# Seven block products in place of eight in an MLP's first matrix product

## The chip, the cores and the metric

The kernel runs on 1 of the 8 cores of one Trainium2 chip. The metric is the device time of one execution in microseconds (us), the median of several runs. TensorE is called PE in the profile, with PEld for its weight loads; VectorE is DVE, ScalarE is ACT, GpSimd is POOL, and SyncE, which issues DMAs, is SP. ACT issues DMAs too.

## The reference

One inference step of one layer over 640 rows (128 context and 512 latent tokens) of 1024 columns, in float32:

```
h    = rmsnorm(x, norm1_g) * (1 + scale1) + shift1
mix  = concat(hgrn2, gla, rglru, short_conv mixers of h @ w_in) @ w_out
x    = x + gate1 * mix
h2   = rmsnorm(x, norm2_g) * (1 + scale2) + shift2
ff   = square(relu(h2 @ mlp_w1)) @ mlp_w2      # 1024 -> 4096 -> 1024
x    = x + gate2 * ff
y    = rmsnorm(x, final_norm_g)
```

The outputs are y and the final states of three mixers. The change is in the part from `gate1 * mix` to the end, above all in `h2 @ mlp_w1`.

## The kernel before

**How a float32 product is formed.** Each operand is split into a rounded part `hi` (type float32r, made by ACT as a copy) and the rest `lo` (made by DVE as a subtraction), and a product is three matmuls, hi*hi, hi*lo and lo*hi, added in PSUM. `prep` (line 108) does this for weights: a DMA from SP brings 128x2048 raw values (1 MB), ACT writes `hi`, DVE writes `lo`. One matmul has a 128x128 stationary operand and 320 or 512 moving columns.

**The stretch before the MLP** (lines 893 to 963). The output projection `op` is formed by row tiles t = 0 to 4 of 128 rows, 48 matmuls each (`out_mm`). For each t, DVE multiplies by the gate (`gm`, line 939) and adds to the residual row `xr[t]`, which stays in SBUF in five buffers to the end; ACT and DVE normalise it (`rms_rstd`), PE transposes it (line 944), and DVE and ACT apply scale and shift and split it into `h2hi` and `h2lo` (lines 950 to 958).

**The MLP** (lines 1007 to 1062) runs in 8 groups g. The first product of a group makes four tiles of 128 of the 4096 hidden columns: for each, `proj_cm` (line 130) issues 8 contraction blocks x 3 terms x 2 halves of 320 rows = 48 matmuls into one PSUM tile of two banks, 192 a group. `relu2` (line 970) takes the finished tile out: ACT Relu from PSUM and Square, DVE square and `lo`. The second product then adds the group's 512 hidden columns into all five row tiles: 5 x 24 = 120 matmuls of 512 columns (line 1043), and DVE adds each finished tile to `acc` (line 1051). In groups 2 to 5, DVE also works out `gate2` from a part of the adaLN weights (line 1001). In the last group `xr += acc * gate2` is made first, and each row tile is then finished, normalised and written out.

**Order.** The framework draws up each engine's instruction order at build time from the program's order and its own estimate of when each instruction is ready; on the chip every engine then works through its own list in that order and waits on semaphores. So is SP's list of DMA issues. `tc.issue_after` ties an instruction behind another on its engine. PSUM holds four tiles of two banks, given out in turn by `mmx`; the weight tiles `wraw` has one buffer, `whi` and `wlo` two each, and `w2raw`, `w2hi`, `w2lo` are the same for the second product.

Of the kernel before, what the change touches and what calls it, by code (L numbers as in the profile page):

```python
# [7 lines left out]
F32 = mybir.dt.float32  # L8
# [45 lines left out]
def hybrid_step_kernel(ctx: ExitStack, tc: tile.TileContext, A: dict, O: dict):  # L54
# [110 lines left out]
    def two(t):  # L165
        return t.rearrange("p (a b) -> p a b", a=2)
# [705 lines left out]
    T2 = ("w2raw", "w2hi", "w2lo")  # L872
# [11 lines left out]
    lq = ctx.enter_context(tc.tile_pool(name="mlpr", bufs=1, side="right", reuse_waits="tile"))  # L884
    stB.close()
# [7 lines left out]
    xr = []  # L893
    for t in range(NCH):
        x = lq.tile([128, D], F32, name=f"xr{t}", tag="xr", bufs=5)
        nc.scalar.dma_start(x, A["x"][128 * t:128 * t + 128, :])
        xr.append(x)
# [3 lines left out]
    for i in (0, 3):  # L901
        wo[i] = prep(A["wout"][i], lp, f"o{i}", tags=T2)
    h2hi = hpool.tile([128, KT, T], F32R, name="h2hi", tag="hhi")
    h2lo = hpool.tile([128, KT, T], F32R, name="h2lo", tag="hlo")
    kord = [4, 5, 0, 1, 2, 3, 6, 7]

    def out_mm(ps, t, ki):
        k = kord[ki]
        ts_ = slice(128 * t, 128 * t + 128)
        hi, lo = (w.rearrange("p (k c) -> p k c", c=D) for w in wo[k // 2])  # L910
        for i, (lh, rh) in enumerate(((oT["hi"], hi), (oT["hi"], lo), (oT["lo"], hi))):
            for n in range(2):
# [11 lines left out]

    for t in range(2):
        pso[t] = mmx(f"op{t}")
# [3 lines left out]
    gate1 = gate_bc("gt1", grow1, lq, nc.sync)  # L930
    for t in range(NCH):
        ts_ = slice(128 * t, 128 * t + 128)
        cnd = 0 if t == 0 else 1
        ps = pso[t]
        if t == NCH - 1:
            g = lp.tile([128, 2048], F32, name=f"gm{t}", tag="w2raw", bufs=1)[:, :D]
        else:
            g = lp.tile([128, D], F32, name=f"gm{t}", tag="big", bufs=2)
        dve.tensor_tensor(g, flat(ps), gate1[:, cnd, :], OP.mult)
        dve.tensor_tensor(xr[t], xr[t], g, OP.add)  # L940
        rs = rms_rstd(lp, xr[t], g, f"b{t}")
        dve.tensor_scalar(g, xr[t], rs, None, op0=OP.mult)
        for k in range(KT):
            pe.transpose(ps[:, k // 4, (k % 4) * 128:(k % 4) * 128 + 128], g[:, 128 * k:128 * k + 128], ident)
        for hf in range(2):
            h2 = lq.tile([128, T], F32, name=f"h2{t}{hf}", tag="r", bufs=2)[:, :512].rearrange("p (k c) -> p k c",
                                                                                               c=128)
            for i in range(4):
                k = 4 * hf + i
                src = ps[:, hf, 128 * i:128 * i + 128]  # L950
                sc, bi = mod["gs2"][:, k, cnd:cnd + 1], mod["sh2"][:, k, cnd:cnd + 1]
                if hf:
                    act.activation(h2[:, i, :], src, AF.Identity, bias=bi, scale=sc)
                else:
                    dve.tensor_scalar(h2[:, i, :], src, sc, bi, op0=OP.mult, op1=OP.add)
            hk = slice(4 * hf, 4 * hf + 4)
            act.activation(h2hi[:, hk, ts_], h2, AF.Copy)
            dve.tensor_tensor(h2lo[:, hk, ts_], h2, h2hi[:, hk, ts_].bitcast(F32), OP.subtract)  # L958
        if t + 2 < NCH:
            out_tile(t + 2)  # L960
        if t == 2:
            for i in range(2):
                w1[i] = prep(A["w1"][i], wpool, f"f{i}", parts=2)

    acc = lp.tile([128, NCH, D], F32, name="acc", tag="ohi")
# [4 lines left out]
    def relu2(f, ps, half=None):  # L970
        r = lq.tile([128, T], F32, name=f"r{f}", tag="r", bufs=2)
        i = f % 4
        act.activation(two(r), ps[:, :, :320], AF.Relu)  # L973
        sq = act.activation(ahi[:, i, :], r, AF.Square)  # L974
        dve.tensor_tensor(r, r, r, OP.mult)  # L975
# [4 lines left out]
    junk = lp.tile([128, 512], F32, name="junk")  # L980
    half2 = const.tile([128, 2, 8], F32, name="half2")

    def silu_rows():
        cb = lq.tile([128, 2, D], F32, name="cb", tag="gate", bufs=1)
        src = A["ccr"]
        nc.sync.dma_start(flat(cb), bass.AP(tensor=src.tensor, offset=src.offset, ap=[[0, 128], [1, 2 * D]]))
        for i in range(4):
            c = slice(512 * i, 512 * i + 512)
            with tc.issue_after(done[0].ins):
                act.activation(junk, flat(cb)[:, c], AF.Sigmoid)  # L990
            dve.tensor_tensor(flat(cb)[:, c], flat(cb)[:, c], junk, OP.mult)
        return cb

    def gate2_part(i, done):
        wt = lp.tile([128, D], F32, name=f"wt{i}", tag="big", bufs=2)
        nc.sync.dma_start(wt, A["ada_g"][i])
        for cnd in range(2):
            for n in range(2):
                c = slice(512 * n, 512 * n + 512)
                with tc.issue_after(done[1].ins):  # L1000
                    dve.scalar_tensor_tensor(junk, wt[:, c], 1.0, cb[:, cnd, c], op0=OP.mult, op1=OP.mult,
                                             accum_out=half2[:, n, cnd:cnd + 1])
# [3 lines left out]

    for g in range(NG):
        for i in range(2 if g else 0):
            w1[2 * g + i] = prep(A["w1"][2 * g + i], wpool, f"f{2 * g + i}", after=done if i else ())
        if g == 0:  # L1010
            pss = []
            for i in range(4):
                pss.append(mmx(f"m1_{i}"))
            for half in range(2):
                for i in range(4):
                    proj_cm(pss[i], w1[i // 2], 128 * (i % 2), 256, h2hi, h2lo, halves=(half,))
            for i in range(4):
                done = relu2(i, pss[i])
        else:
            for i in range(4):  # L1020
                ps = mmx(f"m1_{g}{i}")
                proj_cm(ps, w1[2 * g + i // 2], 128 * (i % 2), 256, h2hi, h2lo)
                done = relu2(4 * g + i, ps)
        for i in range(2):
            w2[2 * g + i] = prep(A["w2"][2 * g + i], lp, f"d{2 * g + i}", tags=T2, parts=1 if g else 2)
        if g == NG - 1:
            for t in range(NCH):
# [68 lines left out]
def _arrays(inp):  # L1096
# [41 lines left out]
    for g, nm in enumerate(("rg_w_r", "rg_w_i")):  # L1138
# [14 lines left out]
        "w1": a["mlp_w1"][0].reshape(8, 128, 16, 256).transpose(2, 1, 0, 3).reshape(16, 128, 2048),  # L1153
        "w2": a["mlp_w2"][0].reshape(16, 2, 128, D).transpose(0, 2, 1, 3).reshape(16, 128, 2048),
# [34 lines left out]
```

## Time and profile before

| | us |
|---|---|
| median of 3 runs (839.96 to 840.07) | 840.04 |
| span of the profiled execution, first to last instruction | 838.3 |
| PE busy in that span | 803.7 (96%) |
| DVE busy | 493.5 (59%) |
| ACT busy | 334.0 (40%) |
| start of the first product of group 0 | 384.51 |
| end of the last matmul of the second product (group 7) | about 828.8 |

The profile is one execution on the chip. The profiled execution's own time is given as its span alone; the runs' median lies 1.7 us above it, the part before the first and after the last instruction. A busy PE is not PE at its peak, since matmuls overlap: the spacing of their starts tells their cost, not their length.

### The profile page before, as it was taken

How to read it: one execution, taken by the hardware profiler on the slowest of the kernel's cores; microseconds unless marked ns; L12 is line 12 of the kernel's file. 1: busy time of each engine (PE TensorE's matmuls, PEld its weight loads, DVE VectorE, ACT ScalarE, POOL GpSimd, SP SyncE). 2: the span in 40 equal slices, each digit the busy share in tenths (PEclk: the TensorE clock that was granted, in tenths of full speed). 3: DMA queues.
4: the chain of work that ended last, by engine and by line, in shares of the span. 5: the costliest groups of instructions: out<-in, count | busy, mean ns of one | idle time of the engine just before them, and what ended most of it. 6: DMA issues, size and time to landing. Idle time of an engine off the chain costs nothing.

```text
span 838.3 us, 13357 instructions
## 1 busy us (share of the span) xinstructions
PE 803.7 (96%) x5728; PEld 712.6 (85%) x5728; DVE 493.5 (59%) x794; ACT 334.0 (40%) x479; POOL 23.2 (3%) x48
## 2 busy tenths in 40 slices
PE   4999999999989999999999999999999999999995
PEld 3798987677777899889989889899898898998984
DVE  4789979776875476356604524645546246457446
ACT  7443459587495322245623403123032131330223
POOL 0040000101010000000000000000000000000001
PEclk9999999999999999999999999999999999999998
DMA  9722233333312434206313212221242222410102
GB/s 362 290 100 103 103 127 119 103 146 85 120 53 97 75 134 174 103 26 226 138 64 108 95 51 101 101 80 72 100 136 91 76 101 77 151 51 1 51 26 100
DMA packets 20732, 90.43 MB, mean 108 GB/s; under 512 B 7232, under 2 KB 8256, under 8 KB 11456
## 3 DMA queue, kind: packets, MB, share of 16 engines
q1 hardware_dynamic: 18720, 85.22, 29.1%
q10 hardware_dynamic: 1440, 4.15, 1.3%
q8 instruction: 45, 0.74, 0.4%
q0 software_dynamic: 512, 0.20, 0.1%
q14 instruction: 15, 0.12, 0.0%
HBM read 86.72 MB, written 2.84 MB: 107 GB/s over the span
## 4 chain that ended last, share of the span: by engine, by line
PE 73%; ACT 11%; DVE 10%; DMA 4%; issue 2%; SPq 0%; ACTq 0%; DVEq 0%
PE m L136 27%; PE m L1043 23%; PE op L913 7%; ACT QbB L106 2%; DMA ar<-in_ada_w_dram 2%; DMA rawo<-in_wout_dram 2%; PE pjcx L136 2%; PE pjdb L136 2%; PE pjbqk L136 1%; PE ap L180 1%; PE rg L775 1%; PE pja L310 1%; PE pjdv L136 1%; ACT QbA L106 1%; PE pjq L310 1%
## 5 line engine op out<-in xcount | busy, mean ns | idle before, releaser
L1043 PE MATMUL m<-hid,aa 128*128 128x512 f32 x632 | 170.7, 389 | 0.0
L1043 PEld LDWEIGHTS m<-hid,aa 128*128 128x128 f32 x632 | 118.3, 188 | 24.2
L136 PE MATMUL m<-h2lo,hif 128*128 128x320 f32 x512 | 122.0, 309 | 0.0
L136 PE MATMUL m<-h2hi,lof 128*128 128x320 f32 x512 | 121.9, 309 | 0.0
L136 PE MATMUL m<-h2hi,hif 128*128 128x320 f32 x512 | 121.5, 309 | 0.0
L106 ACT ACTIVATE hid<-rawd 128x2048 fp32r<-128x2048 f32 (+1 forms) x18 | 30.9, 1723 | 171.3 <-PE m L1043 120.9
L1043 PE MATMUL m<-lod,aa 128*128 128x512 f32 x316 | 97.6, 389 | 0.0
L136 PEld LDWEIGHTS m<-h2hi,hif 128*128 128x128 f32 x512 | 87.2, 188 | 0.5
L136 PEld LDWEIGHTS m<-h2lo,hif 128*128 128x128 f32 x512 | 86.9, 188 | 0.2 <-DVE h2lo L958 0.2
L136 PEld LDWEIGHTS m<-h2hi,lof 128*128 128x128 f32 x512 | 86.9, 188 | 0.0
L127 DVE TENSOR_TENSOR lod<-rawd,hid 128x2048 fp32r<-128x2048 f32 (+1 forms) x18 | 36.9, 2055 | 78.9 <-ACT hid L106 78.9
L1043 PEld LDWEIGHTS m<-lod,aa 128*128 128x128 f32 x316 | 59.3, 188 | 12.4
L975 DVE TENSOR_TENSOR r<-r 128x640 f32<-128x640 f32 x32 | 26.3, 822 | 67.3 <-ACT aa L974 67.3
L1051 DVE TENSOR_TENSOR acc<-m,acc 128x1024 f32<-128x1024 f32 x30 | 36.6, 1220 | 40.0 <-PE m L1043 40.0
L973 ACT ACTIVATE r<-m 128x640 f32<-128x640 f32 x32 | 22.3, 697 | 77.0 <-PE m L136 77.0
L127 DVE TENSOR_TENSOR lof<-rawf,hif 128x2048 fp32r<-128x2048 f32 (+1 forms) x18 | 36.9, 2052 | 24.7 <-ACT hif L106 24.6
L106 ACT ACTIVATE hif<-rawf 128x2048 fp32r<-128x2048 f32 (+1 forms) x18 | 30.9, 1720 | 31.3 <-PE m L136 25.6
L976 DVE TENSOR_TENSOR aa<-r,aa 128x640 fp32r<-128x640 f32 x32 | 26.4, 825 | 1.0
L913 PE MATMUL op<-hio,olo 128*128 128x512 f32 x80 | 24.9, 391 | 0.0
L913 PE MATMUL op<-hio,ohi 128*128 128x512 f32 x80 | 24.8, 391 | 0.0
L913 PE MATMUL op<-loo,ohi 128*128 128x512 f32 x80 | 24.7, 389 | 0.0
L180 PE MATMUL ap<-ar,scx 128*32 128x256 f32 x320 | 21.9, 383 | 2.8 <-DMA ar<-in_ada_w_dram 2.3
(411 smaller groups left out, 1425.1 us busy)
## 6 DMA issues: line engine op xcount, KB each, us to landing
ar<-in_ada_w_dram SPq DMA_DIRECT2D x20, 1024.0 KB, 4.9
rawf<-in_w_dram SPq DMA_DIRECT2D x16, 1024.0 KB, 4.9
rawd<-in_w_dram SPq DMA_DIRECT2D x16, 1024.0 KB, 4.8
rawo<-in_wout_dram SPq DMA_DIRECT2D x4, 1024.0 KB, 4.8
wt<-in_ada_g_dram SPq DMA_DIRECT2D x8, 512.0 KB, 3.5
x<-in_x_dram SPq DMA_DIRECT2D x5, 512.0 KB, 6.5
xr<-in_x_dram ACTq DMA_DIRECT2D x5, 512.0 KB, 7.0
rawa<-in_win_dram SPq DMA_DIRECT2D x2, 1024.0 KB, 9.0
```

What stands on the lines that cost most here:

```text
L106: act.activation(out, src, AF.Copy)
L127: dve.tensor_tensor(lo[:, c], raw[:, c], hi[:, c].bitcast(F32), OP.subtract)
L136: pe.matmul(ps[:, n, :320], wt[:, k, c0:c0 + 128], h[:, k, s], start=(k == 0 and wt is hi and h is hhi), stop=stop)
L180: pe.matmul(ps[32 * g:32 * g + 32, :256], scx[:, 4 * j + g, 2 - 2 * vi:34 - 2 * vi], r3[:, 4 * j + g, :], start=(vi == 0 and j == 0), stop ...
L310: pe.matmul(d, w[:, k, 128 * j:128 * j + 128], (hlo if hi_ else hhi)[:, k, c], start=begin, stop=end, skip_group_check=(ch == "q" and i == 1))
L775: pe.matmul(ps, wrg[:, dl, j, g, :], xc[:, hN * n:hN * n + hN], start=True, stop=True)
L913: ins = pe.matmul(ps[:, n, :], lh[:, k, ts_], rh[:, k % 2, 512 * n:512 * n + 512], start=(ki == 0 and i == 0), stop=(ki == 7 and i == 2))
L973: act.activation(two(r), ps[:, :, :320], AF.Relu)
L975: dve.tensor_tensor(r, r, r, OP.mult)
L976: return sq, dve.tensor_tensor(alo[:, i, :], r, ahi[:, i, :].bitcast(F32), OP.subtract)
L1043: pe.matmul(flat(ps)[:, c], lh[:, i, ts_], rh[:, i % 2, c], start=(i == 0 and pi == 0), stop=(i == 3 and pi == 2))
L1051: dve.tensor_tensor(y, flat(ps), y, OP.add)
```

## The change

The first product becomes one level of Strassen's scheme in Winograd's form. The transposed weights X (hidden columns by contraction) and the transposed rows Y (contraction by tokens) are cut into 2x2 blocks: hidden columns into halves of 2048, the contraction into halves of 512, the 640 tokens into halves of 320. For each of 16 units u, a pair of hidden tiles (tile u of each half), seven products of 4 x 3 = 12 matmuls of 320 columns take the place of eight. The operands of the products are X11, X12, X22 and the sums S1 = X21 + X22, S2 = S1 - X11, S3 = X11 - X21, S4 = X12 - S2, and Y11, Y21, Y22 and T1 = Y12 - Y11, T2 = Y22 - T1, T3 = Y22 - Y12, T4 = Y21 - T2. DVE forms the sums, in place on the raw values where it can; every operand is then split into hi and lo by itself, in pieces of 128x512. Products are added up in PSUM where they follow one another, and ACT and DVE take partial sums out in between (`unit`).

Other parts: the X operands have eight slots in the two buffers of `whi` and `wlo`, and are made up to eight products ahead (`ahead`); the first two products of units 0 to 3, which need only the first 320 tokens, are formed first (`EARLY`), for which halves of the raw weights are loaded once more; the weights w_out (two of four) and w2 come in halves of 512 KB through one buffer of 128x1024; `gm` has one buffer; the residual rows are loaded into two buffers, written to DRAM after the first residual sum and read back in the last group into the space of Y; the MLP's `Relu` and `Square` on ACT become one DVE instruction and an ACT copy; the program's scratch for software DMA is 4096.

```diff
+    def load_x(t):
+        xr[t] = lp.tile([128, D], F32, name=f"xr{t}", tag="big", bufs=2)
+        nc.scalar.dma_start(xr[t], A["x"][128 * t:128 * t + 128, :])
     for i in (0, 3):
-        wo[i] = prep(A["wout"][i], lp, f"o{i}", tags=T2)
...
+        for h in range(2):
+            c = slice(1024 * h, 1024 * h + 1024)
+            raw = lp.tile([128, 1024], F32, name=f"rawo{i}{h}", tag="w2raw", bufs=1)
+            nc.sync.dma_start(raw, A["wout"][i][:, c])
+            cp(f"hi_o{i}", hi[:, c], raw)
+            dve.tensor_tensor(lo[:, c], raw, hi[:, c].bitcast(F32), OP.subtract)
...
+    def split(op, lc, src):
+        act.activation(yhi[op][:, :, lc], src, AF.Copy)
+        dve.tensor_tensor(ylo[op][:, :, lc], src, yhi[op][:, :, lc].bitcast(F32), OP.subtract)
+    names = ("X11", "X12", "S2", "S1", "S3", "S4", "X22")
+    EARLY = 4
+    stream = [(u, n) for u in range(EARLY) for n in names[:2]]
+    for u in range(NU):
+        stream += [(u, n) for n in (names[2:] if u < EARLY else names)]
+    def raw_of(u, early):
...
+            raw = wpool.tile([128, 2, 2, 512], F32, name=f"rawf{u}{'e' if early else ''}", tag="wraw", bufs=1)
...
+    def make_operand():
...
+        if q % 4 == 0:
+            place["hi"] = wpool.tile([128, 2048], F32R, name=f"xh{q}", tag="whi", bufs=2)
+            place["lo"] = wpool.tile([128, 2048], F32R, name=f"xl{q}", tag="wlo", bufs=2)
...
+            if n == "S2":
+                place["S1"] = ls.tile([128, 512], F32, name=f"s1{u}", tag="S1", bufs=1)
+                dve.tensor_tensor(place["S1"], x21, x22, OP.add)
+                dve.tensor_tensor(x21, x11, x21, OP.subtract)
+                dve.tensor_tensor(x11, place["S1"], x11, OP.subtract)
+                dve.tensor_tensor(x12, x12, x11, OP.subtract)
...
+        act.activation(hi, src, AF.Copy)
+        dve.tensor_tensor(lo, src, hi.bitcast(F32), OP.subtract)
+    def ahead(n):
+        while made[0] < min(len(stream), done_products[0] + n, 4 * (done_products[0] // 4 + 2)):
+            make_operand()
+    def product(u, x, y, bank, start):
+        ahead(4)
+        terms = ((xhi[u, x], yhi[y]), (xhi[u, x], ylo[y]), (xlo[u, x], yhi[y]))
+        for k in range(4):
+            for i, (w, h) in enumerate(terms):
+                pe.matmul(bank, w[:, k, :], h[:, k, :], start=(start and k == 0 and i == 0),
+                          stop=(k == 3 and i == 2), skip_group_check=True)
+        done_products[0] += 1
...
-            g = lp.tile([128, D], F32, name=f"gm{t}", tag="big", bufs=2)
+        g = lp.tile([128, 1024], F32, name=f"gm{t}", tag="w2raw", bufs=1)
+        nc.scalar.dma_start(x1d[t], x1)
...
+        if c0 < HT:
+            for op, ks in (("Y11", slice(0, 4)), ("Y21", slice(4, 8))):
+                split(op, slice(c0, e), h2[:, ks, c0:e])
...
+        if c1 > HT:
+            dve.tensor_tensor(y11, y12, y11, OP.subtract)
+            dve.tensor_tensor(t3, y22, y12, OP.subtract)
+            dve.tensor_tensor(y12, y22, y11, OP.subtract)
+            split("T2", lc, y12)
+            split("T1", lc, y11)
+            split("T3", lc, t3)
+            dve.tensor_tensor(y21, y21, y12, OP.subtract)
+            split("Y22", lc, y22)
+            split("T4", lc, y21)
...
+    def relu2(i, r):
+        dve.scalar_tensor_tensor(r, r, 0.0, r, op0=OP.max, op1=OP.mult)
+        sq = act.activation(ahi[:, i, :], r, AF.Copy)
         return sq, dve.tensor_tensor(alo[:, i, :], r, ahi[:, i, :].bitcast(F32), OP.subtract)
+    def unit(u, i):
+        if u >= EARLY:
+            first_products(u)
...
+        act.activation(r0[:, :HT], pa_, AF.Copy)
+        dve.tensor_tensor(r0[:, :HT], pb_, r0[:, :HT], OP.add)
+        product(u, "S2", "T2", pa_, False)
+        act.activation(r0[:, HT:], pa_, AF.Copy)
+        product(u, "S1", "T1", pb_, True)
+        act.activation(r1[:, HT:], pb_, AF.Copy)
+        product(u, "S3", "T3", pa_, False)
+        dve.tensor_tensor(r1[:, HT:], pa_, r1[:, HT:], OP.add)
+        product(u, "S4", "Y22", pb_, False)
+        dve.tensor_tensor(r0[:, HT:], pb_, r0[:, HT:], OP.add)
+        relu2(i, r0)
+        product(u, "X22", "T4", pa_, False)
+        act.activation(r1[:, :HT], pa_, AF.Copy)
+        return relu2(i + 1, r1)
...
         if g == 0:
+            for u in range(EARLY):
+                first_products(u)
+        for i in range(2):
+            done = unit(2 * g + i, 2 * i)
+        for i in range(2):
+            load_w2(2 * g + i)
+        ahead(8)
         if g == NG - 1:
+            xa = hpool.tile([128, NCH, D], F32, name="xa", tag="hhi")
+            for t in range(NCH):
+                xr[t] = xa[:, t, :]
+                nc.scalar.dma_start(xr[t], x1d[t])
```

## Rows read from the trace of the kernel before

**Rows 1.** The page, first part: busy us (share of the span) and instructions.
```profile
PE 803.7 (96%) x5728; PEld 712.6 (85%) x5728; DVE 493.5 (59%) x794; ACT 334.0 (40%) x479; POOL 23.2 (3%) x48
```

**Rows 2.** The chain that ended last: start us, us, engine, tile, line, instructions.
```profile
384.51 8.06 PE m L136 x55
392.57 1.05 PE op L944 x8
...
413.90 27.23 PE m L1043 x120
441.13 28.16 PE m L136 x192
...
801.56 5.48 PE m L1043 x24
```

**Rows 3.** Windows: stretch, us, busy of each engine, clock, DMA share, GB/s.
```profile
496.51:524.66 28.15, 28.15 (x193) 28.15 (x193) 12.04 (x10) 7.93 (x8) 0.00 (x0) 1.00 0.31 113
524.66:551.89 27.23, 27.23 (x123) 22.53 (x122) 15.30 (x32) 5.17 (x4) 0.00 (x0) 1.00 0.23 78
```

**Rows 4.** Groups by line and shape: busy us, mean ns of one, idle before.
```profile
L1051 DVE TENSOR_TENSOR acc<-m,acc 128x1024 f32<-128x1024 f32 x30 | 36.6, 1220 | 40.0 <-PE m L1043 40.0
...
L127 DVE TENSOR_TENSOR lof<-rawf,hif 128x2048 fp32r<-128x2048 f32 x14 | 32.1, 2290 | 23.4 <-ACT hif L106 23.3
...
L106 ACT ACTIVATE hif<-rawf 128x2048 fp32r<-128x2048 f32 x14 | 26.7, 1909 | 26.1 <-PE m L136 25.6 <-DMA rawf<-in_w_dram 0.5
L976 DVE TENSOR_TENSOR aa<-r,aa 128x640 fp32r<-128x640 f32 x32 | 26.4, 825 | 1.0
...
L973 ACT ACTIVATE r<-m 128x640 f32<-128x640 f32 x32 | 22.3, 697 | 77.0 <-PE m L136 77.0
...
L958 DVE TENSOR_TENSOR h2lo<-h,h2hi 128x512 fp32r<-128x512 f32 x10 | 6.9, 690 | 6.8 <-ACT h2hi L957 6.8
...
L957 ACT ACTIVATE h2hi<-h 128x512 fp32r<-128x512 f32 x10 | 6.3, 630 | 18.4 <-DVE h L955 18.3
```

**Rows 5.** DMA issues: count, KB each, median us from issue to landing.
```profile
rawf<-in_w_dram SPq DMA_DIRECT2D x16, 1024.0 KB, 4.9
...
wt<-in_ada_g_dram SPq DMA_DIRECT2D x8, 512.0 KB, 3.5
...
xr<-in_x_dram ACTq DMA_DIRECT2D x5, 512.0 KB, 7.0
```

**Rows 6.** Timeline of ACT and DVE at the start of a first-product stretch.
```profile
560.31 0.69 ACT L973 ACTIVATE r<-m 128x640 f32<-128x640 f32 x1
...
560.44 2.29 DVE L127 TENSOR_TENSOR lod<-rawd,hid 128x2048 fp32r<-128x2048 f32 x1 [5.86 <-ACT hid L106]
562.65 0.82 DVE L975 TENSOR_TENSOR r<-r 128x640 f32<-128x640 f32 x1
```

**Rows 7.** Timeline of PE after a pause, ahead of the MLP.
```profile
293.91 0.87 PE L136 MATMUL pjdv<-hhi,hidv 128*128 128x320 f32 x2 [2.30 <-DVE sgb L457]
294.58 0.73 PE L136 MATMUL pjdv<-hlo,hidv 128*128 128x320 f32 x2
295.12 0.73 PE L136 MATMUL pjdv<-hhi,lodv 128*128 128x320 f32 x2
```

**Rows 8.** Window around that pause, columns as in rows 3.
```profile
292.00:296.00 4.00, 2.09 (x8) 2.12 (x9) 2.01 (x3) 0.00 (x0) 0.00 (x0) 0.69 0.84 346
```

**Rows 9.** Timeline of DVE where the normalised rows are made.
```profile
346.97 1.23 DVE L939 TENSOR_TENSOR gm<-op,bcgt 128x1024 f32<-128x1024 f32 x1 [14.37 <-PE op L913]
...
383.67 1.23 DVE L939 TENSOR_TENSOR gm<-op,bcgt 128x1024 f32<-128x1024 f32 x1 [2.41 <-PE op L913]
384.81 1.36 DVE L955 TENSOR_SCALAR h<-op,gs,sh 128x128 f32<-128x128 f32 x4
```

**Rows 10.** Timeline of DVE in the last group.
```profile
807.06 1.22 DVE L1053 TENSOR_TENSOR acc<-m,bcgt 128x1024 f32<-128x1024 f32 x1 [2.27 <-PE m L1043]
...
824.43 1.22 DVE L1053 TENSOR_TENSOR acc<-m,bcgt 128x1024 f32<-128x1024 f32 x1
```

More of the change, by code (lines that the diff above doesn't have):

```diff
@@ L891, in mmx @@
         return mmtile((psA, psC)[pst[0] % 2], nm)
[L893 to L897, printed above, removed]
+    xr, x1d = {}, {}
+    def load_x(t):
+        xr[t] = lp.tile([128, D], F32, name=f"xr{t}", tag="big", bufs=2)
+        nc.scalar.dma_start(xr[t], A["x"][128 * t:128 * t + 128, :])
+    load_x(0)
+    load_x(1)
     wo = {}
@@ L913, in out_mm @@
                 ins = pe.matmul(ps[:, n, :], lh[:, k, ts_], rh[:, k % 2, 512 * n:512 * n + 512],
-                          start=(ki == 0 and i == 0), stop=(ki == 7 and i == 2))
+                                start=(ki == 0 and i == 0), stop=(ki == 7 and i == 2))
         return ins
-    w1, w2 = {}, {}
     pso = {}
@@ new lines, in hybrid_step_kernel @@
+    EARLY = 4
+    stream = [(u, n) for u in range(EARLY) for n in names[:2]]
+    for u in range(NU):
+        stream += [(u, n) for n in (names[2:] if u < EARLY else names)]
+    place, raws, xhi, xlo = {}, {}, {}, {}
+    made = [0]
+    def raw_of(u, early):
+        key = (u // 2, "e") if early else u
+        if key not in raws:
+            raw = wpool.tile([128, 2, 2, 512], F32, name=f"rawf{u}{'e' if early else ''}", tag="wraw", bufs=1)
+            for i in range(2 if early else 1):
+                if early:
+                    nc.sync.dma_start(flat(raw[:, i]), A["w1"][u + i][:, 0:1024])
+                else:
+                    nc.sync.dma_start(raw.rearrange("p a b c -> p (a b c)"), A["w1"][u])
+            raws[key] = raw
+        return raws[key]
@@ new lines, in make_operand @@
+    def make_operand():
+        q = made[0]
+        if q == len(stream):
+            return
+        made[0] += 1
+        u, n = stream[q]
+        if q % 4 == 0:
+            place["hi"] = wpool.tile([128, 2048], F32R, name=f"xh{q}", tag="whi", bufs=2)
+            place["lo"] = wpool.tile([128, 2048], F32R, name=f"xl{q}", tag="wlo", bufs=2)
+        c = slice(512 * (q % 4), 512 * (q % 4) + 512)
+        hi, lo = place["hi"][:, c], place["lo"][:, c]
+        early = q < 2 * EARLY
+        R = raw_of(u, early)
+        if early:
+            src = R[:, u % 2, names.index(n)]
+        else:
+            x11, x12, x21, x22 = R[:, 0, 0], R[:, 0, 1], R[:, 1, 0], R[:, 1, 1]
+            if n == "S2":
[4 more added lines that the diff above has]
+                dve.tensor_tensor(x12, x12, x11, OP.subtract)
+            src = {"X11": x11, "X12": x12, "S2": x11, "S1": place.get("S1"), "S3": x21, "S4": x12, "X22": x22}[n]
+        act.activation(hi, src, AF.Copy)
+        dve.tensor_tensor(lo, src, hi.bitcast(F32), OP.subtract)
+        xhi[u, n], xlo[u, n] = (x.rearrange("p (k c) -> p k c", c=128) for x in (hi, lo))
@@ L925, in hybrid_step_kernel, with first_products @@
+    w2 = {}
+    psu, ru = {}, {}
+    def first_products(u):
+        psu[u] = mmx(f"mu{u}")
+        product(u, "X11", "Y11", psu[u][:, 0, :HT], True)
+        product(u, "X12", "Y21", psu[u][:, 1, :HT], True)
     for t in range(2):
```

106 lines of the change are left out of this document (58 added, 48 removed).

## The prediction

> **What bounds the kernel now.** I read the page first: PE is busy for 96% of the span and DVE for 59% [rows 1], so PE is the suspect, but a share is an average over stages. The chain that ended last settles it for the stage in question. From the start of the first product at 384.51 it is PE without a gap: in every group 192 matmuls in 28.16 us and then 120 in 27.23 us, down to the last group's second product at 801.56 [rows 2]. No eviction, weight or DMA ends a wait there. The reader should see in the windows that the other engines have room: in the two stretches of one group DVE works 12.04 and 15.30 us, ACT 7.93 and 5.17 us, at full clock [rows 3]. So a matmul taken from the first product is worth its spacing, 28.16/192 = 146.7 ns, as long as nothing else starts to end waits. After the last matmul only some 9 us of tail follow, which the change does not touch.
>
> **What is removed.** A unit has 7 x 12 = 84 matmuls where two tiles had 96; a group has 168 where it had 192. Over 8 groups 192 matmuls go, which is one group's first product: 28.16 us [rows 2]. The number of columns (320) and of weight loads per matmul is as before, so I take the spacing as unchanged. [...] The floor of the group is then 24.64 + 27.23 = 51.87 us, where it was 55.39.
>
> **What is added on VectorE.** For a piece of 128x512 a subtraction costs 0.69 us [rows 4]; four pieces cost 2.76 us where one of 2048 cost 2.29 [rows 4]. A unit needs seven `lo` pieces and four sums: 11 x 0.69 = 7.6 us, where two tiles had 2.29. It needs three additions of 320 columns out of PSUM; no row has that shape, and they lie between 320/1024 of 1.22 us and the 0.69 of 512 [rows 4]: 0.38 to 0.69, I take 0.5, so 1.5 us. The square and the `lo` of two tiles cost 4 x 0.825 = 3.3 us [rows 4], as before. With the group's w2 halves, 4 x 1.22 us (the row of 1024 columns [rows 4]), DVE has 2 x 12.4 + 4.9 = 29.7 us to do for the first product, whose matmuls last 24.64 us. The second product adds five accumulations, 6.1 us, so DVE has about 36 of 51.9 us, and 42 in the groups with gate2 work. That fits only because `ahead` lets up to eight pieces be made while the second product runs.
>
> **What is added on ScalarE.** Seven copies of 0.63 us replace one of 2048, and four copies of 320 columns from PSUM (between half of 0.697 and 0.63 us [rows 4]; I take 0.45) replace two Relus. With four copies of 640 columns (0.7) and four w2 halves (half of a copy of 2048 is about 1) a group comes to some 19 us. That is hidden under 51.9 us of PE.
>
> **Where waits can appear.** Before, a tile of PSUM stood finished until its buffer came round again, tiles later. Now a product adds into a bank from which a partial sum must first be copied out, and the handover has one product of 12 matmuls, 1.76 us, to hide in. A copy of 0.45 or an addition of 0.5 fits if it starts at once. What queues behind what is told by the timeline: the tile's Relu was finished by 561.0, but DVE began its square only at 562.65, directly behind a 2.29 us subtraction that itself had waited 5.86 us for a split [rows 6]. In this engine's list an eviction stands behind such work. Before, this cost nothing. Now more than 1.2 us of it stops PE.
>
> (a) *The start.* DVE, from 383.67: the last `gm` and its sum 2.45, the scale and shift of two row tiles 2.72 [rows 9], four early pieces 2.76, the three sums, the fourth and five `lo` of row tile 3, 9 x 0.69 = 6.2, those of tile 2 that had to wait for the space of `ohi` about 0.8, normalising 0.9, then three sums and T2 of tile 4, 2.76, and the four sums and split of the first S2, 3.45: 22.0 us, to 405.7. Instructions back to back overlap by almost 0.1 us, which some 30 of them bring to 403. PE has 96 early matmuls and the last transposes, 14.1 + 1.05 us, until 399.6 [rows 2]. It waits 3.5 to 6, I take 4.5. Then unit 1: the raw weights have one buffer, so their DMA of 4.9 us [rows 5] starts when unit 0's last operand is split, 5.5 to 6 us after its S2, and S2 of unit 1 needs four sums and a split more, 3.5 us. That is 14 us after PE started unit 0's own five products of 8.8 us: another wait of 4 to 6, I take 4.5. [...] Two such pauses add 2.6. Sum 11.5; bounds 4 (DVE's list is better filled than I think) and 17.
>
> (b) *Groups 3, 5, 7.* The pieces' slots go by fours. 28 products are done when group 2 starts and eight pieces are ready; 42 when group 3 starts and only six are, since 42 is no multiple of four. There the seventh, X22, waits for two products (3.5 us), is split by 5.1, and only then is the raw buffer free: landing at 10.1 [rows 5], X11 and X12 split, four sums, S2 split at 16.1 with DVE to itself and near 18 with the evictions and squares between. S2 is due at 9 x 1.76 = 15.8. I take 1.5 us each, 4.5; bounds 0 and 7.
>
> (c) *Handovers elsewhere.* I take 0.5 us for each of the groups 1 to 7, 3.5. Below, 0; above, 1 us for each of 14 units, 14.
>
> (d) *The end.* The rows parked in DRAM are read back when Y's space falls free, with the last unit's S4 product, 1.8 us before the second product. Five DMAs issued together took 7.0 us in the median [rows 5], so the last sums of 1.22 us end about 9 to 10 us into the second product, where DVE wanted to finish row tile 0 at 5.5 (807.06). It works tile 3 at 824.43 [rows 10], 1 us after that tile's matmuls end, so most of this is caught up. The five issues also stand in ACT's list ahead of the last unit's final copy, which the second product needs for its third and fourth hidden tile. I take 1; bounds 0 and 3.
>
> **What costs nothing.** The w_out halves need four passes of load, copy and subtraction, 3.5 + 1 + 1.2 us [rows 4, 5], where two took 4.9 + 1.9 + 2.3: they are ready some 4.7 us later, inside the 14.37 us for which DVE then waits for PE [rows 9]; without that cover they cost up to 4.7. The row loads and stores stand in ACT's list, each load behind the store of the row two tiles before it, two row tiles ahead of need. The w2 halves take 24 us of such passes in a group of 52; uncovered, a few us a group, which the range holds. Parking writes and early reloads are 7 MB beside a DMA share of 0.2 to 0.3 [rows 3].
>
> **The sum.** -28.2 + 11.5 + 4.5 + 3.5 + 1 = -7.7. On the profile's span of 838.3 that is 830.6; with the 1.7 us by which the median lies above the span, 840.04 - 7.7 = **832.3**. The bounds of (a) to (d) give 4 to 41 us of cost, 816 to 853.
>
> **The rivals.** *All hidden.* DVE's 36 to 42 us in 51.9 speaks for it; the start chain, which counts only work that PE needs, against it. Costs of 3 to 6 us: 815 to 818. *VectorE becomes the bound of the first product* (the other side). Place: the 24.64 us of each group's first product. If its list puts the 29.7 us there and leaves the second product empty, each of groups 1 to 7 loses 5.1 us, 35 in all, and with 12.5 for start and end the time is 860; with half of that, 842. It decides from (28.16 - 12.5)/7 = 2.2 us lost per group. For it: the fixed order and rows 6. Against it: eight slots. I price it at 850. [...] *No difference*, the costs adding up to 28 within 0.2% (1.7 us, about what a measurement of this kernel can tell from none). That the matmuls are not removed can't be: their number is fixed by the program.
>
> **Chances.** Some waits, 820 to 838: 0.44. All hidden: 0.23. No difference: 0.06. VectorE bound: 0.24. Clock: 0.03. So faster 0.67, same 0.06, slower 0.27. The likeliest case's own range is 824 to 838. The range for 8 in 10 cuts the upper part of the VectorE case with the clock's, and half of "all hidden": 815 to 851.
>
> **What would show it.** Right: 168 matmuls in 24.6 to 26 us in groups 2, 4, 6, up to 2 us more in 3, 5, 7; pauses before S2 of units 0 and 1 with the lower clock behind them; DVE busy near 610 us. Wrong: gaps of PE before every product that wait for DVE or ACT evictions (VectorE bound); no pause around 400 to 420 (all hidden); another spacing than 146.7 ns; PE waiting in the last second product on row tiles read back.

## The result and the profile after

The changed kernel takes 883.08 us (median of 4 runs, 882.23 to 884.64) where the kernel before, run on the same chip, took 840.0: 1.051 times as long, interval 1.0499 to 1.0528. I had forecast 832.3 us, with a range up to 851. The profiled execution has a span of 882.0 us, against 838.3 before. The 192 matmuls are gone, 28.2 us, so some 72 us of waiting have come in: 882.0 - (838.3 - 28.2) = 71.9.

Line numbers from here on are those of the changed kernel: L1005 is a matmul of the first product, L1182 one of the second, L1093 to L1105 are the copies and sums that empty the accumulators of a unit in the order of the code, L1148 and L1149 copy and split a half of w2, L989 and L990 a piece of w1. The page, first part, and its row of the granted clock in 40 slices:

```profile
PE 806.4 (91%) x5536; PEld 697.5 (79%) x5536; DVE 595.3 (67%) x1040; ACT 378.6 (43%) x631; POOL 24.3 (3%) x48
...
PEclk9999999999999999997999999989999899699798
```

PE is busy longer with fewer matmuls (806.4 us for 5536, 803.7 for 5728 in [rows 1]), and the row of the clock, at 9 in every slice up to the MLP, falls in it again and again. DVE has 100 us more to do, as I had reckoned (595 for "near 610"). The windows tell whether that is too much; the columns are those of [rows 3], and the stretches are the first products of groups 0 (its end), 2, 3 and 6:

```profile
408.00:441.60 33.60, 30.09 (x171) 27.48 (x172) 27.96 (x44) 18.36 (x32) 0.00 (x0) 0.94 0.31 113
...
510.30:545.00 34.70, 32.35 (x196) 29.30 (x195) 20.55 (x30) 15.06 (x25) 0.00 (x0) 1.00 0.27 91
566.40:606.40 40.00, 35.74 (x201) 32.45 (x200) 23.70 (x35) 15.94 (x26) 0.00 (x0) 0.91 0.30 106
...
743.00:787.00 44.00, 35.41 (x194) 32.20 (x193) 20.57 (x29) 14.48 (x25) 0.00 (x0) 0.84 0.26 96
```

In the stretch of group 3 DVE works 23.70 of 40.00 us and ACT 15.94. Neither is full, and yet PE waits. For whom, the view of waits says (engine, line <- releaser: us in total, times, longest), for PE from 376 us to the end; for the kernel before the same view has not one row:

```profile
PE mu L1005 <- DVE ra L1094: 18.3, 9, 7.4
PE op L1037 <- DVE gm L1035: 6.2, 2, 5.7
PE mu L1005 <- ACT h L1044: 5.4, 2, 3.1
PE mu L1005 <- ACT ra L1096: 4.8, 8, 1.2
PE mu L1005 <- ACT rb L1098: 3.5, 5, 1.4
PE mu L1005 <- DVE rb L1100: 2.7, 5, 1.2
```

The rows of L1037 and L1044 belong to the start (below). The other four are evictions, and each is of a kind that the code does not need. S2 adds into accumulator `pa`, but waits for L1094, which reads `pb`; S1 restarts `pb`, but waits for L1096, which reads `pa`; S3 and S4 in turn wait for L1098 and L1100, which read the other one. The chain shows it in group 2, where [rows 2] had 192 matmuls in one piece:

```profile
516.46 1.07 ACT hid L1148
...
517.55 1.23 DVE lod L1149
518.78 0.41 DVE ra L1094
...
519.23 2.03 PE mu L1005 x12
...
521.29 0.45 ACT ra L1096
...
521.78 1.91 PE mu L1005 x11
```

From one product's start to the next there are 2.55 us in place of 1.76: the end of the last matmul, the eviction of 0.45 and its release stand in full between them. In the second unit of a group three matmuls of the second product (0.69 us) stand in most handovers, and little is lost there. And before the first handover, the first eviction has waited in the list of its engine. The timeline of group 3 (start, duration, engine, line; in brackets the idle time before and what ended it):

```profile
567.36 1.23 DVE L1149 TENSOR_TENSOR lod<-rawd,hid 128x1024 fp32r<-128x1024 f32 x1 [2.59 <-ACT hid L1148]
...
568.61 6.60 SPq L1147 DMA_DIRECT2D rawd<-in_w_dram  x2
...
572.54 1.06 ACT L1148 ACTIVATE hid<-rawd 128x1024 fp32r<-128x1024 f32 x1 [5.21 <-DMA rawd<-in_w_dram]
573.50 0.42 ACT L1093 ACTIVATE ra<-mu 128x320 f32<-128x320 f32 x1
573.63 1.23 DVE L1149 TENSOR_TENSOR lod<-rawd,hid 128x1024 fp32r<-128x1024 f32 x1 [3.42 <-ACT hid L1148]
...
574.77 0.48 DVE L1094 TENSOR_TENSOR ra<-mu,ra 128x320 f32<-128x320 f32 x1
...
575.31 0.56 PE L1005 MATMUL mu<-r,xh 128*128 128x320 f32 x2 [2.84 <-DVE ra L1094]
```

The products that L1093 and L1094 read from were done at 572.47. But on ACT the second w2 half stands ahead of L1093, and that half can be loaded only when the first is split and the one raw buffer is free. So ACT is idle for 5.21 us with work behind it in its list, DVE for 3.42, and PE for 2.84. After this pause the clock is down (window, columns as before):

```profile
575.31:585.00 9.69, 8.64 (x38) 7.79 (x38) 2.46 (x3) 3.26 (x6) 0.00 (x0) 0.65 0.62 218
```

0.65 is a mean: from 576.40 to 579.50 the clock is 0.50, and S2 and S1 take 2.98 and 3.56 us for 12 matmuls in place of 1.76. After the 1.01 us pause of group 2 the window from 519.20 to 529.00 has a clock of 1.00. A pause with such a fall of the clock stands once a group in groups 3, 5, 6 and 7 (pauses of 2.65 to 7.37 us, clock 0.84 to 0.91 over the stretch), and in groups 2 and 4 there is none (1.00 over the stretch). Among the chances this is *Clock*, to which I had given 3 in 100.

**Where the 71.8 us are.** From the timeline of PE I take the end of each group's last first-product matmul. Group 1's is at 489.4. By [rows 2] it was at 413.90 + 55.39 = 469.3; without the 48 matmuls that are gone by then (7.04), with the 17 of the second product that now stand among group 1's last products (3.9), it would be 466.1: 23.3 us lost. Groups 2 to 7 take 360.2 us from there, where 6 x 51.87 = 311.2: 49.0 lost. What follows takes 32.4 us, where 103 matmuls of the second product and 9.5 us of tail are 32.9: nothing lost. So the rows parked in DRAM cost nothing at the end: the landing in the chain (848.47 to 852.95) makes DVE late, not PE, and it catches up. Reckoned another way, PE was idle for 43.9 us between 384.5 and 849.65 (465.15 us, busy 421.23), and busy for 38.9 us while the clock stood at 0.50; at half the speed that cost some 19 us, an estimate. The rest, some 9 us, is not traced.

### The profile page after: what moved, and what is told of

Read it like the earlier page. It is cut to its first block, busy times and chain, and to the rows that moved or that the text cites. A ratio compares the mean times of both kernels' runs of the same rounds, so it can differ in the third digit from the quotient of the medians.

```text
span 882.0 us, 13446 instructions
## 1 busy us (share of the span) xinstructions
PE 806.4 (91%) x5536; PEld 697.5 (79%) x5536; DVE 595.3 (67%) x1040; ACT 378.6 (43%) x631; POOL 24.3 (3%) x48
## 4 chain that ended last, share of the span: by engine, by line
PE 60%; DVE 15%; ACT 13%; DMA 8%; issue 2%; POOLq 0%; SPq 0%; ACTq 0%; DVEq 0%
PE m L1182 19%; PE mu L1005 18%; PE op L922 5%; DMA rawd<-in_w_dram 3%; DVE lod L1149 2%; ACT QbB L106 2%; PE pjdv L136 2%; PE pjcx L136 2%; PE pjdb L136 2%; ACT hid L1148 2%; PE pja L310 2%; DMA rawo<-in_wout_dram 1%; DMA rowgt<-gt 1%; PE ap L180 1%; PE pjbqk L136 1%
## 5 line engine op out<-in xcount | busy, mean ns | idle before, releaser
L1182 PE MATMUL m<-hid,aa 128*128 128x512 f32 x632 | 174.1, 390 | 0.1
L1182 PEld LDWEIGHTS m<-hid,aa 128*128 128x128 f32 x632 | 117.3, 188 | 23.5 <-DVE aa L1085 0.7
L1005 PE MATMUL mu<-yhhi,xh 128*128 128x320 f32 x256 | 87.1, 342 | 14.5 <-ACT h L1044 5.4
L1182 PE MATMUL m<-lod,aa 128*128 128x512 f32 x316 | 100.1, 390 | 0.0
L1149 DVE TENSOR_TENSOR lod<-rawd,hid 128x1024 fp32r<-128x1024 f32 x32 | 39.1, 1223 | 85.0 <-ACT hid L1148 85.0
L1148 ACT ACTIVATE hid<-rawd 128x1024 fp32r<-128x1024 f32 x32 | 33.9, 1058 | 136.4 <-PE m L1182 86.2
L1005 PE MATMUL mu<-r,xh 128*128 128x320 f32 x256 | 64.0, 338 | 21.9 <-DVE ra L1094 18.3
L1005 PE MATMUL mu<-yhlo,xh 128*128 128x320 f32 x256 | 83.3, 325 | 0.0
L1005 PE MATMUL mu<-yhhi,xl 128*128 128x320 f32 x256 | 82.5, 324 | 0.0
L989 ACT ACTIVATE xh<-rawf 128x512 fp32r<-128x512 f32 x88 | 52.6, 625 | 57.0 <-DMA rawf<-in_w_dram 29.3
L1005 PEld LDWEIGHTS mu<-yhhi,xh 128*128 128x128 f32 x256 | 51.8, 203 | 25.3 <-ACT ra L1096 9.6
L1005 PEld LDWEIGHTS mu<-r,xh 128*128 128x128 f32 x256 | 45.8, 204 | 28.7 <-DVE ra L1094 20.9
L1182 PEld LDWEIGHTS m<-lod,aa 128*128 128x128 f32 x316 | 59.1, 188 | 11.6
L990 DVE TENSOR_TENSOR xl<-rawf,xh 128x512 fp32r<-128x512 f32 x88 | 58.3, 686 | 4.7 <-ACT xh L989 4.7
L1005 PEld LDWEIGHTS mu<-yhlo,xh 128*128 128x128 f32 x256 | 52.1, 204 | 0.4
L1005 PEld LDWEIGHTS mu<-yhhi,xl 128*128 128x128 f32 x256 | 51.5, 202 | 0.0
L1005 PE MATMUL mu<-r,xl 128*128 128x320 f32 x128 | 42.3, 331 | 1.3 <-DVE xl L990 1.1
L1005 PE MATMUL mu<-t,xh 128*128 128x320 f32 x128 | 29.0, 313 | 0.0
L1005 PEld LDWEIGHTS mu<-r,xl 128*128 128x128 f32 x128 | 26.3, 205 | 1.9 <-DVE xl L990 1.8
L1100 DVE TENSOR_TENSOR rb<-mu,rb 128x320 f32<-128x320 f32 x16 | 7.9, 491 | 27.0 <-PE mu L1005 26.8
```

Source lines behind the costliest of these rows:

```text
L989: act.activation(hi, src, AF.Copy)
L990: dve.tensor_tensor(lo, src, hi.bitcast(F32), OP.subtract)
L1005: pe.matmul(bank, w[:, k, :], h[:, k, :], start=(start and k == 0 and i == 0), stop=(k == 3 and i == 2), skip_group_check=True)
L1148: act.activation(hi[:, c], raw, AF.Copy)
L1149: dve.tensor_tensor(lo[:, c], raw, hi[:, c].bitcast(F32), OP.subtract)
L1182: pe.matmul(flat(ps)[:, c], lh[:, i, ts_], rh[:, i % 2, c], start=(i == 0 and pi == 0), stop=(i == 3 and pi == 2))
```

## The experiments

Two theories were to be told apart. T1: a product waits for the eviction of the other accumulator, because both lie in one PSUM tile and the wait is kept for the tile. T2: evictions come late, because they stand behind w2 halves that wait for their DMA. The rival from before: VectorE has too much to do. The table at the end has all times; the kernel before, run beside each of them, took 839.65 to 840.04 us.

**Two tiles.** The first pair goes together; two tiles for a unit need all of PSUM with two units, so the control has the smaller lead as well.

```
-    EARLY = 4
+    EARLY = 2                         # both kernels
-        psu[u] = mmx(f"mu{u}")        # from here the second alone
-        product(u, "X11", "Y11", psu[u][:, 0, :HT], True)
-        product(u, "X12", "Y21", psu[u][:, 1, :HT], True)
+        psu[u] = [mmx(f"mua{u}"), mmx(f"mub{u}")]
+        product(u, "X11", "Y11", psu[u][0][:, 0, :HT], True)
+        product(u, "X12", "Y21", psu[u][1][:, 0, :HT], True)
```

> Only the number of units whose X11 and X12 products run ahead of the loop goes from 4 to 2; the tile with both banks stays. It is the control for the next kernel, which needs this. All theories: the waits at the handovers stay as they are; at the start PE has 48 matmuls (7 us) less to do while VectorE prepares unit 0, and it does them later. Between 880 and 893 us.

> As the control, but the two accumulators of a unit lie in two PSUM tiles in place of the two banks of one tile, so that a product waits only for the copy or sum that reads its own accumulator. Theory T1 (the wait is kept for the whole tile, so each of the five handovers of a unit shows an eviction of 0.6 to 0.8 us in full, 16 x 5 x 0.7 = 56 us with what the clock loses behind it): products at 1.76 us in place of 2.55, 40 to 55 us less than the control, 830 to 845. Theory T2 (evictions stand in the lists of ScalarE and VectorE behind w2 halves that wait for their DMA): S2 still waits 3 to 7 us at the start of a group, 10 to 20 us less at most, 863 to 875. VectorE as the bound: no change, since its work is the same.

The control takes 894.92 us (ratio 1.0658, 1.0634 to 1.0681), 12 more than the changed kernel and a little above the range: the units ahead were worth more than I thought. Two tiles take 857.31 (1.0213, 1.0178 to 1.0248), 37.6 less than the control, 2.4 short of what T1 asked. The absolute figure (830 to 845) is missed by 12 us, by as much as the control is longer than the changed kernel. The chain of group 2:

```profile
515.46 1.75 PE mua L1005 x12
517.21 1.76 PE mub L1005 x12
518.97 1.76 PE mua L1005 x12
520.73 1.76 PE mub L1005 x12
522.49 1.76 PE mua L1005 x12
```

Every product starts 1.76 us after the one before, with the same evictions. T1 holds. The copy that the code has between two products of one accumulator falls here into the product of the other, and the 12 matmuls still take 1.75 to 1.76 us: reading the one PSUM tile did not slow the matmuls into the other.

**w2 halves between the evictions.** 4 units ahead and one tile with two banks as in the changed kernel; the loads are spread over the units, each half held behind evictions.

```
+        s = dve.tensor_tensor(r0[:, :HT], pb_, r0[:, :HT], OP.add)
         product(u, "S2", "T2", pa_, False)
+        load_w2(u, 0, act.activation(r0[:, HT:], pa_, AF.Copy), s)     # behind L1096 and L1094
...
+        load_w2(u, 1, dve.tensor_tensor(r0[:, HT:], pb_, r0[:, HT:], OP.add))    # behind L1102
...
-            load_w2(2 * g + i)                                         # both halves, behind the unit loop
```

> As the changed kernel (4 units ahead, one tile with two banks), but the four w2 halves of a group are loaded and split between the evictions of its two units, each held behind an eviction that precedes it. T2: the waits of 3 to 7 us for the first eviction of groups 1 to 7 go, with the lower clock behind them: 25 to 40 us less, 843 to 858. T1: the handovers of 0.6 to 0.8 us stay, 5 to 20 us less, 863 to 878. VectorE as the bound: no change, 880 to 886.

858.78 us (1.0228, 1.0212 to 1.0244), 24.3 less; all of it in groups 2 to 7, 336.0 us for 360.2. That is 0.7 short of what T2 asked, and the clock of group 3 is 1.00 again. The handovers stay. The longest pause left in group 3 is 1.70 us, for an eviction (here L1109) that stands in VectorE's list behind the split of a piece of w1:

```profile
573.51 0.69 DVE L990 TENSOR_TENSOR xl<-rawf,xh 128x512 fp32r<-128x512 f32 x1 [2.80 <-ACT xh L989]
574.12 0.48 DVE L1109 TENSOR_TENSOR ra<-mu,ra 128x320 f32<-128x320 f32 x1
...
574.66 0.56 PE L1005 MATMUL mu<-r,xh 128*128 128x320 f32 x2 [1.70 <-DVE ra L1109]
```

The chain then goes on through the wait that I had called (b), for w1's raw buffer, but at its end PE has hardly waited (busy 9.28 of 9.34 us from 579.76 to 589.10):

```profile
574.23 5.76 DMA rawf<-in_w_dram
...
580.02 0.69 DVE s L984
580.71 1.27 DVE xl L990 x2
...
582.58 0.41 DVE rb L1115
...
583.03 6.25 PE mu L1005 x40
```

**Both edits**, on the two-tile kernel.

> Both edits together. T1 and T2 each true in part: first product of a group 25 to 27 us, clock near 1.00 in the MLP, 815 to 830 us, below the kernel before. If VectorE's list is the bound behind them, not under 840.

844.47 us (1.0057, 1.0038 to 1.0075): not under the kernel before, the figure that the rival asked. But groups 2 to 7, where VectorE was to be the bound, do what was expected of the two causes (321.0 us); the start, with two units ahead, ends 20 us late. So the next kernels keep four units ahead and take both accumulators out of one tile in another way: every PSUM tile of this part holds one bank.

```
-    psC = ctx.enter_context(tc.tile_pool(name="psC", bufs=2, space=PS, reuse_waits="tile"))
+    stA.close()                       # the older pool of two-bank tiles
+    psC = ctx.enter_context(tc.tile_pool(name="psC", bufs=8, space=PS, reuse_waits="tile"))
     def mmx(nm):
-        return mmtile((psA, psC)[pst[0] % 2], nm)
+        return [psC.tile([128, 512], F32, name=f"{nm}{n}", tag="mm") for n in range(2)]
```

> The changed kernel with 4 units ahead as it was, but every PSUM tile of the output projection and the MLP holds one bank, so the two accumulators of a unit are two tiles (evictions of 1024 columns become two of 512). T1 alone, without the change in the number of units ahead that the two-tile kernel needed: as much less than the changed kernel as the two-tile kernel had against its control, 30 to 45 us, 838 to 853. T2 as the main cause: 10 us or less, 873 to 883.

> One-bank tiles and the w2 halves between the evictions, 4 units ahead. If the two causes and the start add up: the kernel with both edits and 2 units ahead (844) less the 7 to 12 us that two units more ahead of the start are worth, 832 to 838. If the start is bound by VectorE's list whatever PE has to do meanwhile: 842 to 846.

One-bank tiles alone: 842.35 us (1.0028, 1.0014 to 1.0042), 40.7 less than the changed kernel. With the w2 halves between the evictions: 832.95 (0.9917, 0.989 to 0.9945), 50.1 less and 0.8% faster than the kernel before. The two gains alone make 65.0, together 50.1, so 14.9 us go with either edit. The first S2 of a group fits that: it waits for L1094 only through the tile, and L1094 is late only through the list. With one-bank tiles alone no pause over 0.8 us is left in groups 2, 4 and 5, and one each of 1.37, 5.77 and 1.45 us in groups 3, 6 and 7. The chain of this kernel in group 2:

```profile
501.67 17.59 PE mu L1007 x120
519.26 0.23 PE m L1187
519.50 7.17 PE mu L1007 x48
526.66 27.38 PE m L1187 x119
```

168 matmuls in 24.8 us, without a gap, with DVE at 16.94 of 24.99 us in that window. VectorE's work is what it was in the changed kernel (594.7 us against 595.3); its amount was not the bound.

**The kernel before with w2 in halves.**

```
+        for h in range(2):
+            raw = lp.tile([128, 2048], F32, name=f"rawd{j}{h}", tag="w2raw", bufs=1)[:, :1024]
+            nc.sync.dma_start(raw, A["w2"][j][:, c])
+            act.activation(hi[:, c], raw, AF.Copy)
+            dve.tensor_tensor(lo[:, c], raw, hi[:, c].bitcast(F32), OP.subtract)
```

> The kernel before with one part of the change alone: w2 loaded, copied and split in halves through one buffer of 1024 columns. T2 in its plain form (the halves cost wherever they are): 6 to 25 us slower, 846 to 865. If it is the queueing of evictions that PE waits for behind them, which before has slack of a whole tile: within 2 us of 840.

839.87 us (1.0, 0.9989 to 1.0011). The halves cost nothing where an eviction has a tile's time to wait, so the edit is not slow by itself; it is the two together.

**The start.** In the changed kernel the products' operands are late. The chain there (`op` L1037 are the transposes of row tiles t = 3 and t = 4):

```profile
387.61 1.11 PE op L1037 x8
...
390.11 1.13 DVE gm L1030
391.24 0.60 DVE h L1067
...
396.10 1.14 DVE xr L1031
...
402.04 0.68 DVE gm L1035
...
402.76 1.98 PE op L1037 x8
```

The last transposes come at 402.76, where [rows 2] had 392.57. Between `gm` of t = 4 and its residual sum, L1031, stand eight sums and splits of t = 3. PE can't use the time, though the last 24 of the 96 early matmuls are still to do: they belong to unit 3, whose PSUM tile is the one in which t = 4 is transposed, and wait until it is emptied (L1044; unit 2 had waited 2.32 us for the tile of t = 3):

```profile
407.79 0.64 PE L1005 MATMUL mu<-yhhi,xh 128*128 128x320 f32 x1 [3.06 <-ACT h L1044]
```

And `gm` of t = 4 is itself late. In the kernel before it began at 383.67 [rows 9], as soon as its matmuls were done; here these are done at 380.76, but it begins at 390.02, behind the transposes of t = 3, which read the one buffer that `gm` has. No run gives it a second buffer, so what that costs stays open.

Four kernels ask what VectorE's list costs here. The first changes the order on the kernel with 832.95 us (and sends the last gate's rows through GpSimd's queue); the other three stand each on the first: less work, sums on GpSimd, t = 4 first.

```
-            split("T3", lc, t3)                       # and the lines for Y22 and T4 below it
+            late.append((lc, t3, y12, y21, y22))      # they follow behind the loop over t
...
-        gate2 = gate_bc("gt2", gate_rows("gt2", nc.sync), lq, nc.sync)
+        gate2 = gate_bc("gt2", gate_rows("gt2", nc.gpsimd), lq, nc.gpsimd)
```

> As the kernel before it in this list, and the splits of T3, Y22 and T4 of the third and fourth row tiles wait until the fifth is normalised (4.4 us of VectorE's list behind S2 of unit 0 in place of ahead of it), and the rows of the last gate go through GpSimd's queue in place of SyncE's, where the w2 loads of group 6 stand behind them. If the order of VectorE's list at the start and the queue cost what the traces show, 4 and 6 us less: 824 to 832. If not, 832 to 838.

829.54 us (0.9873, 0.9852 to 0.9895), the fastest here. That is 3.4 us less by medians, but both profiled executions have a span of 829.1, so how much of it is the edit stays unclear. By the table the start ends 2.3 us earlier, and groups 2 to 7 take 2.2 more. The queue gave nothing, since group 6 still waits (2.79 us for one copy).

```
-            dve.tensor_tensor(y11, y12, y11, OP.subtract)      # and the other sums, and the splits of T1, T3, T4
-        product(u, "S1", "T1", pb_, True)
+        product(u, "S1", "T2", pb_, True)                      # likewise S3; X22 reads Y22
```

> From the kernel with the other start order. Left out: the sums and splits of T1, T3 and T4 at the start (T2 is a plain copy of one quarter, and the products read T2 or Y22 in their place), so that the output is not the reference's; VectorE's list is some 10 us shorter there, and nothing else changes. If what is left of the loss, some 12 to 13 us at the start, is VectorE's list: 7 to 11 us less, 818 to 823. If it is the loads of the raw weights through their one buffer, or PE's work itself: within 2 us of 829.5.

826.62 us (0.9852, 0.9826 to 0.9878), 2.9 less: a miss for both. Ten us off the list gave three. PE still waits 4.0 us for the normalised rows of t = 4.

```
+            en = dve if t == NCH - 1 else pool
+            en.tensor_tensor(y11, y12, y11, OP.subtract)       # and the two sums behind it
...
+                en = pool if u < 2 else dve
+                en.tensor_tensor(place["S1"], x21, x22, OP.add)    # and the three behind it
```

> From the same kernel, nothing left out: the three sums of Y for the third and fourth row tiles and the four sums of the weights of units 0 and 1 go to GpSimd in place of VectorE, 14 instructions, some 8.5 us by VectorE's durations. If VectorE's list is the bound at the start and GpSimd's sums fit beside it: 821 to 826. If they are much slower there, or slow VectorE down (the one row of a GpSimd sum of 1024 columns, 3.2 us, is nearly three times VectorE's 1.2): 829 to 836.

839.7 us (0.999, 0.9979 to 1.0001), 10 more. The timeline says why, GpSimd first, VectorE below:

```profile
390.78 1.78 POOL L1074 TENSOR_TENSOR t<-h 128x512 f32<-128x512 f32 x1
392.64 1.61 POOL L1075 TENSOR_TENSOR h<-h 128x512 f32<-128x512 f32 x1
394.21 2.24 POOL L987 TENSOR_TENSOR s<-rawf 128x512 f32<-128x512 f32 x1
```

```profile
393.04 2.30 DVE L1036 TENSOR_TENSOR xr<-xr,gm 128x1024 f32<-128x1024 f32 x1
395.26 1.74 DVE L944 TENSOR_TENSOR r<-h,r 128x512 fp32r<-128x512 f32 x1
...
402.55 0.68 DVE L993 TENSOR_TENSOR xl<-rawf,xh 128x512 fp32r<-128x512 f32 x1
```

While GpSimd's sums run, the same split takes VectorE 1.74 us, and 0.68 when they are done.

```
+                if t > 2:
+                    st.enter_context(tc.issue_after(xsum.ins))     # the sums of t = 3 behind L1031 of t = 4
```

> From the kernel with the other start order, nothing left out: the sums of Y of the fourth row tile are held behind the residual sum of the fifth, so that the fifth is normalised and transposed earlier. If what PE lacks at the start is the fifth row tile (PE waited 6.0 us for its normalised rows), its transposes come 3 to 4 us earlier and the kernel takes 825 to 828. If the sum of VectorE's list up to the first S2 is what counts, whatever its order: 828 to 831.5.

829.86 us (0.9876, 0.986 to 0.9893): no change, but the edit did not do what it was to do. t = 4's transposes come 0.3 us earlier (396.86 for 397.20), not 3 to 4, since the build also moved those of t = 3 back (386.70 for 385.34). PE then waits 0.73 us for an operand of S2, for which it did not wait before, and the chain is DVE in one piece from 390.64 to 406.51. That fits both things binding at once, t = 4 and the operands of S2; it is not shown. I have not tried both together, so what the rest of the start would give stays open.

All times in us. "End of g1" and "g2 to g7" are the end of group 1's last first-product matmul and the time from there to group 7's, from the timelines of PE. They do not hold quite the same matmuls: by the end of g1, 10 to 20 of group 1's second product (0.23 us each) are done in the changed kernel and the four below it, which have two-bank tiles, none in the others, and "g2 to g7" has 10 or 11 more in the six with one-bank tiles:

| kernel | median | span | end of g1 | g2 to g7 |
|---|---|---|---|---|
| before | 840.0 | 838.3 | 469.3 | 332.3 |
| changed | 883.08 | 882.0 | 489.4 | 360.2 |
| 2 units ahead (control) | 894.92 | 891.5 | 499.3 | 358.7 |
| 2 ahead, two tiles | 857.31 | 855.3 | 490.3 | 331.0 |
| w2 behind evictions | 858.78 | 859.0 | 491.6 | 336.0 |
| 2 ahead, two tiles, w2 | 844.47 | 840.5 | 485.2 | 321.0 |
| one-bank tiles | 842.35 | 839.5 | 475.6 | 329.1 |
| one-bank tiles, w2 | 832.95 | 829.1 | 473.7 | 321.5 |
| the same, start order | 829.54 | 829.1 | 471.4 | 323.7 |
| ... less work on T (not the output) | 826.62 | 824.8 | 467.2 | 322.6 |
| ... sums on GpSimd | 839.7 | 838.7 | 480.9 | 323.8 |
| ... t = 4 first | 829.86 | 829.0 | 472.4 | 322.5 |

## Why the prediction was wrong

**What failed.** Two steps, and that each makes the other dearer: left in alone, they cost 25.8 and 9.4 us, together 50.1.

The first is the sentence that "the handover has one product of 12 matmuls, 1.76 us, to hide in". I read the code: two accumulators, two banks, the one emptied while the other fills. But both banks are one tile of the program, and the waits are kept for tiles (2.55 us from one product's start to the next in one tile, 1.76 in two). So the handover had nothing to hide in, and an eviction of 0.45 us cost 0.5 to 0.8 us of PE even when it started at once. I had asked whether an eviction "fits if it starts at once", and should have asked on what the next matmul waits. The kernel before could not show it: there a tile was filled, emptied and left alone. Undone, it gives back 40.7 us alone, 25.8 (858.78 to 832.95) behind the other edit.

The second stands under "What costs nothing": the w2 halves, "uncovered, a few us a group". They were uncovered. I had seen in [rows 6] that work on w2 stands ahead of an eviction in an engine's list, and that this had waited 5.86 us. I read that as a wait for a split. It was for the copy on ACT, which had waited for its DMA, as a row of the same timeline of the kernel before says:

```profile
558.49 1.91 ACT L106 ACTIVATE hid<-rawd 128x2048 fp32r<-128x2048 f32 x1 [7.37 <-DMA rawd<-in_w_dram]
```

So I priced DVE's durations, not that a list stops while its head waits for a DMA, with the loads of a group strung on one buffer: load 3.9, copy 1.07, split 1.24, load again. Undone, it gives back 24.3 us alone, 9.4 behind the other edit. With the kernel before's slack, it cost nothing (839.87).

**Term by term.** *Removed, 28.16*: right. 120 matmuls in 17.59 us are 146.6 ns each. *VectorE's and ScalarE's added work*: right, evictions at 0.48 and 0.44 for 0.5 and 0.45, busy time 595.

*(a), the start, 11.5, bounds 4 to 17*: 23.3 lost up to the end of group 1, above the bound; the handovers of the first four units were not in it. With the two causes out it is 11.5 (473.7 against 469.3 - 7.04 = 462.2, with no matmul of group 1's second product ahead there). That it is the forecast's own figure is luck in part, since the pauses are others: the sum over VectorE's list set out from 383.67, and the last `gm` began at 390.02; the early matmuls were to cover it, and the last 24 had to wait for t = 4's PSUM tile. PE paused ahead of t = 4's transposes (5.71 us; 9.07 with the causes out), and not ahead of S2 of units 0 and 1. No run shows the 2.6 of the 11.5, a lower clock behind two pauses ahead of these. In its place the changed kernel has the clock at 0.50 from 391.80 to 394.60 and from 407.80 to 411.30, behind the pauses of 2.32 and 3.06 us for L1044, with matmuls 0.27 us apart in place of 0.15. In the kernel before, the pairs of matmuls behind the one pause of [rows 7] start 0.54 us apart, where ahead of it they started 0.29 apart.

For (b) and (c) I count the second product's matmuls that stand in each of groups 2 to 7 (117, 126, 114, 126, 114 and 124 in the changed kernel, 226.9 ns each) and not 120 for all. *(b), 1.5 in groups 3, 5 and 7*: 8.3, 8.3 and 9.7 in the changed kernel, mostly by w2, handovers and clock. With the causes out they lose 1.2, 1.3 and 1.0, near the forecast; that they wait for w1's raw buffer there is not shown. *(c), 0.5 a group*: groups 2 and 4 lose 4.3 and 4.2, and 0.8 and 0.3 with the causes out. Group 6 loses 14.0: its w2 loads stood behind a DMA of 10.08 us for the last gate's rows on the way, so S2 waited 7.37. With the causes out it still loses 3.2. *(d), 1*: nothing was lost.

With both causes out, (a) measures 11.5, (b) and (c) 7.8 (321.5 against 311.2 and 2.5 for 11 matmuls more), (d) -0.4: 18.9 us, where I had 20.5. That the time, 832.95, meets the forecast of 832.3 is right for the sizes of these terms, in part by luck, and no credit for the forecast: the kernel that I was asked about has the two causes in it.

**The rivals.** *VectorE bound* had 0.24 and the right sign, by the wrong mechanism: DVE has 40% of a first-product stretch to spare in group 3, and with the same work the kernel runs in 833. Its "fixed order" was half of the truth. *Clock*, pauses of PE with a lower clock behind them, had 0.03: they are real in four groups, one in each (2.65 to 7.37 us); that [rows 3], at full clock, show none says nothing of a kernel with other waits.

## What to carry to other kernels

When two accumulators are to take turns, look at what the wait is kept on: here giving each its own tile (which also made two of each eviction of 1024 columns) was worth 41 us of 883. In a list that is worked in order, an operation that waits for a DMA delays every eviction behind it (here ACT was idle for 5.21 us with one behind it); place it behind the evictions, and price a load, copy and split on one buffer as a chain, not as busy time. A cover seen in the kernel before (a finished tile that lies idle) is part of that kernel; a change that uses up the slack has to be reckoned again with every list that leaned on it.

## What the runs showed of the hardware

Beside sums on GpSimd VectorE was slower: splits of 128x512 took 1.74 us beside them and 0.68 after them, a sum of 1024 columns 2.30 where the same sum took 1.23 in the kernel with the other start order, while two of VectorE's products that read one operand from PSUM went on at 1.28 together. GpSimd was slower too: its sum of 128x512 beside those two products took 1.30 us, the six after it, beside VectorE's splits and sums, 1.59 to 2.24.

In the changed kernel the clock fell to 0.50 in or behind pauses of PE of 2.32 us and more, with 12 matmuls in up to 3.58 us behind them, and stayed at 1.00 after pauses of 1.01 and 0.97 us. The length of the pause alone does not decide it: behind the same pause of 2.32 us at the start, matmuls stood 0.27 us apart in the changed kernel (391.76) and 0.15 apart with w2 behind the evictions (392.71). With less work on T they stood 0.27 apart after 1.90 us (group 6), while with w2 behind the evictions the clock stayed at 1.00 after 1.70.
